# Six of 31 convolution taps as ScalarE products added up in DRAM, and no cleared probability blocks

## The chip, the cores and the metric

One core of one Trainium2 chip runs the whole kernel. Its engines work from queues of their own and meet through semaphores: TensorE (PE, matmuls), VectorE (DVE), ScalarE (ACT), GpSimd (POOL) and the DMA queues, of which SyncE (SP) issues nearly all here. The metric is device time in microseconds. Before the change it is 1760.06 us, the median of 3 runs (1760.02 to 1760.11).

## The reference

One layer of a decoder trunk on 1024 tokens of 1024 channels, all in float32. An input projection feeds two mixers; their gated sum goes through an output projection, and a SwiGLU block follows. What the change touches is the convolution branch and the weighting of the attention:

```python
p = probs(qb1, k1f) - lamf * probs(qb2, k2f)          # causal softmax, twice, per head
return jnp.einsum('bhqk,bhkd->bhqd', p, vf)
...
c = causal_depthwise_conv(u_a * jax.nn.sigmoid(u_b), conv_w[l], conv_b[l])   # width 31, per channel
c = jax.nn.silu(layer_norm(c, conv_ln_w[l], conv_ln_b[l]))
y_b = c @ w_proj_conv[l]
```

Per channel the convolution is a sum of 31 shifted copies of u, each times one number, plus a bias. The probabilities are causal: for a query block i, key blocks above i have weight zero.

## The kernel before

Every float32 matrix product is made of three float32r products (high times high, high times low, low times high; `mm3`, L152 to L154). So each operand is split: ScalarE casts the high part (`split_hi`, L119), VectorE subtracts to get the low part (`split_lo`, L124). `whi` and `wlo` are a weight's parts, made from the loaded `wraw`.

The first stage (`first`, L345) runs projection items one after the other: V (values), U (the two halves of the convolution's input) and the first head's Q. A U item makes one tile of 128 channels of u, as `sg`, and stores it to `u_d[c]` in DRAM. The convolution works on such tiles, c from 0 to 7: `conv_load` (L505) has POOL clear 30 columns of margin at the left of the tile `u` and SP load the rest; `conv_taps` (L514) is one VectorE operation per tap over 128x1024 elements, the first (L519) with the bias, 30 more (L525) that multiply and add into `acc`; SP stores `acc` to `c_d[c]`. There are two buffers of `u` and one of `acc`.

The taps are background work. The list `bg.todo` holds them, and `bg.step` emits a few after each piece of foreground work: 3.25 per yield of an item in the first stage (L764), and in attention as many as each step's slack allows (L970). Load number c goes into the list 31 places before its end (L551), that is, ahead of the taps of the tile before. A scheduler then places the emitted instructions on each engine's queue by its own timing, so the queues are not simply in the order of the source; `after(...)` only keeps an instruction behind another one.

Attention goes through 64 steps of a head and a block of 128 queries. `scores` (L798): PE multiplies into `sc` (three banks, L816 and L817), VectorE adds the bias and finds the minimum (`mn`, L818), ScalarE exponentiates and sums (`l`, L823), VectorE makes two reciprocals (L829, L833) and subtracts the second softmax from the first (L832). `turn` (L836) transposes the probabilities `E` into `pT` (L852) and splits them into `ph` and `pl`, which hold two query blocks, 256 columns, per key block. For the odd key block 2b+1 the first 128 of these columns lie above the diagonal; POOL clears them (L842, L843) in each new tile. `weigh` (L857) multiplies by the values `vh` and `vl` into `pW`, 256 columns for each key block; `back` (L869) turns the result back and scales it by the reciprocal in `RL`. Projection items (`more`, L910) fill PE's queue between these. The pool `a0` of the first stage (`ap`, with four buffers `xt` of x tiles) is closed at L771, and the attention tiles take its room.

The LayerNorm over channels (`ln_chunks`, L1020) loads all `c_d` after attention.

Of the kernel before, what the change touches and what calls it, by code (L numbers as in the profile page):

```python
# [56 lines left out]
def kernel(  # L57
# [456 lines left out]
    def conv_taps(c):  # L514
        acc = []

        def first_tap():
            acc.append(cv.tile([P, S], F32, tag="acc", name=f"acc{c}", bufs=1))
            dve.tensor_scalar(  # L519
                acc[0][:], us[c][:, 0:S], cw[:, c, 0:1], pcol("conv_b", c), op0=ALU.mult, op1=ALU.add  # L520
            )

        def tap(t):
            def go():
                dve.scalar_tensor_tensor(  # L525
                    acc[0][:], us[c][:, t : t + S], cw[:, c, t : t + 1], acc[0][:], op0=ALU.mult, op1=ALU.add
                )
                if t == CW - 1:
                    nc.sync.dma_start(c_d[c][:], acc[0][:])

            return go

        return [first_tap] + [tap(t) for t in range(1, CW)]
# [264 lines left out]
    def scores(h, i):  # L798
# [4 lines left out]
        l = sm.tile([P, 2], F32, tag="l", name=nm("l"))  # L803
        E = []
        qs = slice(i % 4 * P, (i % 4 + 1) * P)
        for j in range(2):
# [4 lines left out]
            for w in SPLITS[i]:  # L811
# [9 lines left out]
                )  # L821
                c0 += w
            act.activation(  # L823
                e[:, :nk], e[:, :nk], AF.Exp, bias=mn[:, j : j + 1], scale=-1.0, accum_out=l[:, j : j + 1]
            )
        if h not in RL:
            RL[h] = sm.tile([P, NT], F32, tag="rl1", name=f"rl1_{h}")
        c = sm.tile([P, 1], F32, tag="rl", name=nm("rl"))
        dve.reciprocal(c[:], l[:, 1:2])  # L829
        dve.scalar_tensor_tensor(c[:], c[:], neglam[:], l[:, 0:1], op0=ALU.mult, op1=ALU.mult)  # L830
        e1, e2 = E[0][:, :nk], E[1][:, :nk]
        dve.scalar_tensor_tensor(e1, e2, c[:], e1, op0=ALU.mult, op1=ALU.add)  # L832
        dve.reciprocal(RL[h][:, i : i + 1], l[:, 0:1])  # L833
        ES[h, i] = E[0]

    def turn(h, i):  # L836

        b = i // 2
        if (h, b) not in PT:
            ph = aps.tile([P, NT, 256], F32R, tag="ph", name=nm("ph"), bufs=1)  # L840
            pl = aps.tile([P, NT, 256], F32R, tag="pl", name=nm("pl"), bufs=1)
            pool.memset(f32(ph[:, 2 * b + 1, 0:P]), 0.0)  # L842
            pool.memset(f32(pl[:, 2 * b + 1, 0:P]), 0.0)  # L843
            PT[h, b] = ph, pl
        ph, pl = PT[h, b]
        e = ES.pop((h, i))
        qs = slice((i % 2) * P, (i % 2 + 1) * P)
        for k0 in range(0, i + 1, 4):
            n = min(4, i + 1 - k0)
            pt = pm("pT")  # L850
            for k in range(n):
                pe.transpose(pt[:, k * P : (k + 1) * P], e[:, (k0 + k) * P : (k0 + k + 1) * P], ident[:])  # L852
# [16 lines left out]
    def back(h, b, ar):  # L869
# [6 lines left out]
        jk = sm.tile([P, VD], F32, tag="jk", name=nm("jk"), bufs=1)  # L876
        for e in range(2):
            i = 2 * b + e
            src, r = pt[:, e * P : (e + 1) * P], RL[h][:, i : i + 1]
            act.activation(AN[h][:, i, :], src, AF.Identity, scale=r)  # L880
            act.activation(jk[:], src, AF.Square, scale=r, accum_out=SSA[h][:, i : i + 1])

# [638 lines left out]
```

## Time and profile before

| | us |
|---|---|
| median of the runs | 1760.06 |
| the profiled execution's own time | 1761.41 |
| its span in the profile | 1759.6 |
| VectorE busy in the span | 1273.2 |
| ScalarE busy in the span | 800.5 |

The span is one execution as the hardware profiler saw it, with 1.8 us of the execution's time outside. A row of a view gives busy time and the mean duration of one instruction; "idle before" is the time in which the engine stood still ahead of the instructions of that group, with the instruction that ended it. Matmuls are pipelined, so the distance from start to start tells their pace, not the duration in the row. The granted TensorE clock is full in every slice of the page.

### The profile page before, as it was taken

Reading aid. Unit: us, or ns where it says so; the run is one execution under the profiler, and the core shown is the slowest. Engines: PE = TensorE matmul, PEld = TensorE weight load, DVE = VectorE, ACT = ScalarE, POOL = GpSimd, SP = SyncE. Lnnn points to the kernel's source line nnn. Section 1 sums busy time; section 2 is a strip of 40 time slices with the busy share of each in tenths; the row PEclk is TensorE's granted clock in tenths of the full one; section 3 lists DMA queues with packets and bytes.
Section 4 is the critical chain, followed back from the end, with each engine's and each line's share of the span. In section 5 each row is a group of like instructions: output and inputs, shape, how many; then the busy total and the mean of one; then the engine's idle time right before and its main releaser. Section 6 shows DMA issues by size and latency. Waiting matters only on the chain.

```text
span 1759.6 us, 25844 instructions
## 1 busy us (share of the span) xinstructions
PE 1740.3 (99%) x9367; PEld 1503.1 (85%) x9367; DVE 1273.2 (72%) x2187; ACT 800.5 (45%) x1886; POOL 26.7 (2%) x106
## 2 busy tenths in 40 slices
PE   7999999999999999999999999999999999999999
PEld 6898998988999998988888888888888888888887
DVE  6388879999988888886687534877667666664544
ACT  4211241558767776655557313643333333333332
POOL 3000000000000000000000000000000000000000
PEclk9999999999999999999999999999999999999999
DMA  8433353235444344352983544234544544697663
GB/s 248 164 121 114 108 158 124 76 96 151 111 138 124 88 114 138 86 163 76 336 268 108 168 167 144 91 102 146 177 150 158 176 157 139 210 360 242 215 216 131
DMA packets 255728, 275.34 MB, mean 156 GB/s; under 512 B 16064, under 2 KB 177896, under 8 KB 255600
## 3 DMA queue, kind: packets, MB, share of 16 engines
q1 hardware_dynamic: 253568, 267.45, 47.6%
q0 software_dynamic: 1744, 5.19, 1.0%
q8 instruction: 74, 1.21, 0.3%
q10 hardware_dynamic: 288, 1.05, 0.2%
q14 instruction: 54, 0.44, 0.1%
HBM read 176.59 MB, written 78.68 MB: 145 GB/s over the span
## 4 chain that ended last, share of the span: by engine, by line
PE 95%; DMA 2%; ACT 1%; DVE 1%; issue 0%; SPq 0%; ACTq 0%
PE acc L1375 22%; PE pg L153 15%; PE pg L154 15%; PE pg L152 15%; PE acc L451 12%; PE sc L817 2%; PE sc L816 2%; PE wo L154 2%; PE wo L153 2%; PE wo L152 2%; PE pT L852 2%; PE pW L152 1%; PE pW L154 1%; PE pW L153 1%; PE pQ L714 1%; DMA wraw<-in_w_in_dram 1%
## 5 line engine op out<-in xcount | busy, mean ns | idle before, releaser
L525 DVE SCALAR_TENSOR_TENSOR acc<-u,cw,acc 128x1024 f32<-128x1024 f32 x240 | 306.8, 1278 | 2.8
L152 PE MATMUL pg<-whi,hT_hi 128*128 128x256 f32 x768 | 220.3, 287 | 1.2 <-ACT hT_hi L119 1.2
L154 PE MATMUL pg<-whi,hT_lo 128*128 128x256 f32 x768 | 219.8, 286 | 0.4 <-DVE hT_lo L124 0.4
L153 PE MATMUL pg<-wlo,hT_hi 128*128 128x256 f32 x768 | 219.1, 285 | 0.2 <-DVE wlo L124 0.2
L119 ACT CAST whi<-wraw 128x1024 fp32r<-128x1024 f32 x109 | 114.4, 1051 | 215.9 <-PE pg L153 122.1
L152 PE MATMUL pg<-hT_hi,whi 128*128 128x512 f32 x512 | 201.6, 394 | 0.0
L154 PE MATMUL pg<-hT_hi,wlo 128*128 128x512 f32 x512 | 200.9, 393 | 0.0
L153 PE MATMUL pg<-hT_lo,whi 128*128 128x512 f32 x512 | 200.5, 392 | 0.0
L124 DVE TENSOR_TENSOR wlo<-wraw,whi 128x1024 fp32r<-128x1024 f32 x109 | 132.8, 1219 | 70.8 <-ACT whi L119 66.7
L124 DVE TENSOR_TENSOR wlo<-draw,whi 128x1024 fp32r<-128x1024 f32 x75 | 91.8, 1224 | 89.6 <-ACT whi L119 84.3
L152 PEld LDWEIGHTS pg<-whi,hT_hi 128*128 128x128 f32 x768 | 147.7, 192 | 4.2 <-ACT hT_hi L119 2.5
L154 PEld LDWEIGHTS pg<-whi,hT_lo 128*128 128x128 f32 x768 | 147.8, 192 | 2.3 <-DVE hT_lo L124 1.1
L153 PEld LDWEIGHTS pg<-wlo,hT_hi 128*128 128x128 f32 x768 | 147.7, 192 | 2.0 <-DVE wlo L124 0.5
L119 ACT CAST whi<-draw 128x1024 fp32r<-128x1024 f32 x75 | 79.1, 1055 | 129.5 <-PE acc L451 125.9
L451 PE MATMUL acc<-wlo,whi 128*128 128x512 f32 x308 | 119.8, 389 | 0.0
L451 PE MATMUL acc<-whi,wlo 128*128 128x512 f32 x308 | 119.8, 389 | 0.0
L823 ACT ACTIVATE E<-E,mn 128x256 f32<-128x256 f32 (+7 forms) x128 | 99.7, 779 | 35.8 <-DVE mn L818 33.6
L154 PEld LDWEIGHTS pg<-hT_hi,wlo 128*128 128x128 f32 x512 | 96.2, 188 | 19.0
L153 PEld LDWEIGHTS pg<-hT_lo,whi 128*128 128x128 f32 x512 | 96.2, 188 | 18.7
L152 PEld LDWEIGHTS pg<-hT_hi,whi 128*128 128x128 f32 x512 | 96.3, 188 | 18.3
L1375 PE MATMUL acc<-h_hi,whi 128*128 128x512 f32 x240 | 93.4, 389 | 0.0
L1375 PE MATMUL acc<-h_lo,whi 128*128 128x512 f32 x240 | 93.4, 389 | 0.0
(270 smaller groups left out, 3951.5 us busy)
## 6 DMA issues: line engine op xcount, KB each, us to landing
wraw<-in_w_gate_up_dram SPq DMA_DIRECT2D x44, 512.0 KB, 4.8
wraw<-in_w_in_dram SPq DMA_DIRECT2D x40, 512.0 KB, 4.5
qs<-qs SPq DMA_DIRECT2D x96, 128.0 KB, 2.3
wd<-in_w_down_dram SPq DMA_DIRECT2D x44, 256.0 KB, 3.1
tdT<-wd SPq DMA_DIRECT2D x88, 128.0 KB, 4.3
draw<-sdS SPq DMA_DIRECT2D x44, 256.0 KB, 3.8
draw<-tdT SPq DMA_DIRECT2D x44, 256.0 KB, 3.9
wraw<-in_w_in_dram SPq DMA_DIRECT2D x32, 256.0 KB, 3.3
```

Of the source, the lines that this page charges most:

```text
L119: act.copy(dst, src)
L124: last_lo[0] = dve.tensor_tensor(dst, src, f32(hi), op=ALU.subtract).ins
L152: pe.matmul(o, lh, rh, start=start, stop=False)
L153: pe.matmul(o, lh, rl, start=False, stop=False)
L154: last_mm[0] = pe.matmul(o, ll, rh, start=False, stop=stop).ins
L451: m = pe.matmul(o[s_][i][:], l_[:, ts], r_[:, 512:], start=start and j + y_ == 0, stop=j == n - 1 and y_ == 2, skip_group_check=not start,)
L525: dve.scalar_tensor_tensor(acc[0][:], us[c][:, t : t + S], cw[:, c, t : t + 1], acc[0][:], op0=ALU.mult, op1=ALU.add)
L816: pe.matmul(o[:, :w], qh[:, qs], k, start=True, stop=False)
L817: last_mm[0] = pe.matmul(o[:, :w], ql[:, qs], k, start=False, stop=True).ins
L823: act.activation(e[:, :nk], e[:, :nk], AF.Exp, bias=mn[:, j : j + 1], scale=-1.0, accum_out=l[:, j : j + 1])
L852: pe.transpose(pt[:, k * P : (k + 1) * P], e[:, (k0 + k) * P : (k0 + k + 1) * P], ident[:])
L1375: pe.matmul(o[:], a_[x_][:, k, :], b_[y_][:, k, :], start=start and k + x_ + y_ == 0, stop=k == 3 and x_ == 1, skip_group_check=not start,)
```

## The change

For the tiles c = 0 to 4 (`FROM_ACT` = 5), taps 0 to 5 (`ADDED` = 6) are not done by VectorE. ScalarE makes each product in a buffer `part` (of the four `xt` buffers). POOL's queue stores the first one, with the bias, to `c_d[c]`, and adds the others to it with accumulating DMAs. VectorE starts at tap 6, emits one product after every fourth of its taps, and writes its last tap into `u` itself, from where POOL's queue adds it to `c_d[c]`, too. Tiles 5 to 7 keep all their taps on VectorE. The margin of `u` is cleared by VectorE now.

In `weigh` the last key block is multiplied for the second 128 columns alone, so `ph` and `pl` need no cleared block. The sums of the first softmax go straight into `RL`, and one reciprocal is made for two query blocks.

```diff
+    ADDED, FROM_ACT = 6, 5
...
-            pool.memset(u[:, : CW - 1], 0.0)
+            dve.memset(u[:, : CW - 1], 0.0)
             nc.sync.dma_start(u[:, CW - 1 :], u_d[c][:])
...
+        def product(t):
+            with after(last_of(mybir.EngineType.Activation)):
+                part_ = ap.tile([P, S], F32, tag="xt", name=nm("part"), bufs=4)
+                u, w = us[c][:, t : t + S], cw[:, c, t : t + 1]
+                if t == 0:
+                    act.activation(part_[:], u, AF.Identity, scale=w, bias=pcol("conv_b", c))
+                    pool.dma_start(c_d[c][:], part_[:])
+                else:
+                    act.activation(part_[:], u, AF.Identity, scale=w)
+                    pool.dma_start(c_d[c][:], part_[:], accum_op=ALU.add)
...
         def tap(t):
             def go():
-                dve.scalar_tensor_tensor(
-                    acc[0][:], us[c][:, t : t + S], cw[:, c, t : t + 1], acc[0][:], op0=ALU.mult, op1=ALU.add
-                )
+                u, w = us[c][:, t : t + S], cw[:, c, t : t + 1]
+                if t == n_add:
+                    acc.append(cv.tile([P, S], F32, tag="acc", name=f"acc{c}", bufs=1))
+                    if n_add:
+                        dve.tensor_scalar(acc[0][:], u, w, None, op0=ALU.mult)
+                    else:
+                        dve.tensor_scalar(acc[0][:], u, w, pcol("conv_b", c), op0=ALU.mult, op1=ALU.add)
+                else:
+
+                    dst = us[c][:, :S] if t == CW - 1 else acc[0][:]
+                    dve.scalar_tensor_tensor(dst, u, w, acc[0][:], op0=ALU.mult, op1=ALU.add)
+                if (t - n_add) % 4 == 3 and (t - n_add) // 4 < n_add:
+                    product((t - n_add) // 4)
                 if t == CW - 1:
-                    nc.sync.dma_start(c_d[c][:], acc[0][:])
+                    if n_add:
+                        pool.dma_start(c_d[c][:], us[c][:, :S], accum_op=ALU.add)
+                    else:
+                        nc.sync.dma_start(c_d[c][:], us[c][:, :S])
...
-                bg.todo.insert(max(0, len(bg.todo) - CW), conv_load(c))
-                bg.add(conv_taps(c))
+                n_add = ADDED if c < FROM_ACT else 0
+                bg.todo.insert(max(0, len(bg.todo) - CW + n_add), conv_load(c))
+                bg.add(conv_taps(c, n_add))
...
-        dve.reciprocal(RL[h][:, i : i + 1], l[:, 0:1])
+        if i % 2:
+            dve.reciprocal(RL[h][:, 1, i - 1 : i + 1], RL[h][:, 0, i - 1 : i + 1])
...
-            pool.memset(f32(ph[:, 2 * b + 1, 0:P]), 0.0)
-            pool.memset(f32(pl[:, 2 * b + 1, 0:P]), 0.0)
...
-            mm3(o[:, :256], vh[:, k, :], vl[:, k, :], ph[:, k, :], pl[:, k, :], k == 0, k == nkt - 1)
+            q = slice(P if k == nkt - 1 else 0, 256)
+            mm3(o[:, q], vh[:, k, :], vl[:, k, :], ph[:, k, q], pl[:, k, q], k == 0, k == nkt - 1)
```

With 30 taps fewer in the list, the queues come out otherwise. POOL's queue after the bias rows held only clears before, first of `u`, then of `ph` and `pl`:

```order
L677 DMA t_d7_330<-b_d_322 128x1152
L508 MEMSET u2_1485 128x30
L508 MEMSET u3_1869 128x30
L842 MEMSET ph_285_3217 128x128
L843 MEMSET pl_286_3218 128x128
L508 MEMSET u4_2431 128x30
```

Now it holds the stores and accumulations, here from the first of tile 0 to the third of tile 1:

```order
L527 DMA c_d0_160<-part_95_996 128x1024
L530 DMA c_d0_160<-part_97_1030 128x1024
L530 DMA c_d0_160<-part_100_1064 128x1024
L530 DMA c_d0_160<-part_111_1168 128x1024
L530 DMA c_d0_160<-part_115_1230 128x1024
L530 DMA c_d0_160<-part_119_1292 128x1024
L527 DMA c_d1_161<-part_134_1413 128x1024
L530 DMA c_d1_161<-part_136_1448 128x1024
L549 DMA c_d0_160<-u0_949 128x1024
L530 DMA c_d1_161<-part_139_1482 128x1024
```

Each accumulation on one `c_d` waits for the one before it, and tile 0's last (L549) stands behind two transfers of tile 1.

VectorE's queue where one tile's taps end and the next one's begin (`wlo` and `sg` belong to the projection items) read before:

```order
L525 SCALAR_TENSOR_TENSOR acc0_952<-u0_949,cw_114,acc0_952 128x1024 x3
L548 TENSOR_TENSOR sg_130_1453<-pg_131_1458,sg_130_1453 128x512
L124 TENSOR_TENSOR wlo_134_1494<-wraw_132_1491,whi_133_1493 128x1024
L519 TENSOR_SCALAR acc1_1424<-u1_1085,cw_114,pvec_105 128x1024
L525 SCALAR_TENSOR_TENSOR acc1_1424<-u1_1085,cw_114,acc1_1424 128x1024 x5
L548 TENSOR_TENSOR sg_139_1528<-pg_140_1534,sg_139_1528 128x512
```

and reads now:

```order
L544 SCALAR_TENSOR_TENSOR u0_949<-u0_949,cw_114,acc0_952 128x1024
L570 TENSOR_TENSOR sg_133_1410<-pg_135_1418,sg_133_1410 128x512
L538 TENSOR_SCALAR acc1_1369<-u1_1094,cw_114 128x1024
L544 SCALAR_TENSOR_TENSOR acc1_1369<-u1_1094,cw_114,acc1_1369 128x1024 x2
L124 TENSOR_TENSOR wlo_131_1382<-wraw_129_1379,whi_130_1381 128x1024
L544 SCALAR_TENSOR_TENSOR acc1_1369<-u1_1094,cw_114,acc1_1369 128x1024
L510 MEMSET u2_1512 128x30
L544 SCALAR_TENSOR_TENSOR acc1_1369<-u1_1094,cw_114,acc1_1369 128x1024 x2
```

The last tap goes into `u0`, and the clear of `u2`, in the same buffer, follows after four taps and two other operations.

At the start of attention, where VectorE's first score reduction (L818 before, L844 now, `E` from `sc` and `tb0`) stands in its queue, the taps before it belonged to tile 4:

```order
L525 SCALAR_TENSOR_TENSOR acc4_2876<-u4_2431,cw_114,acc4_2876 128x1024
L548 TENSOR_TENSOR sg_254_2980<-pg_255_2985,sg_254_2980 128x512
L818 ISA E_258_3036,mn_256_3034<-sc_259_3037,tb0_3032 128x128
L818 ISA mn_256_3034 128x1
L818 ISA E_260_3042,mn_256_3034<-sc_261_3043,tb0_3032 128x128
```

Now tile 4 is done, tile 5 has begun, and the clear of `u6` stands just ahead:

```order
L544 SCALAR_TENSOR_TENSOR u4_2064<-u4_2064,cw_114,acc4_2681 128x1024
L540 TENSOR_SCALAR acc5_2972<-u5_2823,cw_114,pvec_105 128x1024
L124 TENSOR_TENSOR wlo_279_2986<-wraw_277_2982,whi_278_2985 128x1024
L544 SCALAR_TENSOR_TENSOR acc5_2972<-u5_2823,cw_114,acc5_2972 128x1024
L233 TENSOR_TENSOR neglam_130<-lsum_132 128x1
L544 SCALAR_TENSOR_TENSOR acc5_2972<-u5_2823,cw_114,acc5_2972 128x1024
L510 MEMSET u6_2969 128x30
L234 TENSOR_SCALAR neglam_130<-neglam_130 128x1
L544 SCALAR_TENSOR_TENSOR acc5_2972<-u5_2823,cw_114,acc5_2972 128x1024
L570 TENSOR_TENSOR sg_284_3074<-pg_285_3079,sg_284_3074 128x512
L844 ISA E_288_3131,mn_286_3128<-sc_289_3132,tb0_3126 128x128
```

The reductions write `E` into a buffer of `part`, and the loads of `vh0`, `vl0` and `tb0` on SP go into such buffers, too.

More of the change, by code (lines that the diff above doesn't have):

```diff
@@ L512, in conv_load, with conv_taps @@
         return go
-    def conv_taps(c):
+    def conv_taps(c, n_add):
         acc = []
[L517 to L520, printed above, removed]
-            )
+        def product(t):
[8 more added lines that the diff above has]
+                    pool.dma_start(c_d[c][:], part_[:], accum_op=ALU.add)
         def tap(t):
             def go():
-                dve.scalar_tensor_tensor(
-                    acc[0][:], us[c][:, t : t + S], cw[:, c, t : t + 1], acc[0][:], op0=ALU.mult, op1=ALU.add
-                )
+                u, w = us[c][:, t : t + S], cw[:, c, t : t + 1]
[10 more added lines that the diff above has]
+                    product((t - n_add) // 4)
                 if t == CW - 1:
-                    nc.sync.dma_start(c_d[c][:], acc[0][:])
+                    if n_add:
+                        pool.dma_start(c_d[c][:], us[c][:, :S], accum_op=ALU.add)
+                    else:
+                        nc.sync.dma_start(c_d[c][:], us[c][:, :S])
             return go
-        return [first_tap] + [tap(t) for t in range(1, CW)]
+        return [tap(t) for t in range(n_add, CW)]
     hT_hi = big.tile([P, NKT, S], F32R, tag="xhi", name="hT_hi")
@@ L802, in scores @@
         mn = sm.tile([P, 2], F32, tag="mn", name=nm("mn"))
-        l = sm.tile([P, 2], F32, tag="l", name=nm("l"))
+        l = sm.tile([P, 1], F32, tag="l", name=nm("l"))
+        if h not in RL:
+            RL[h] = sm.tile([P, 2, NT], F32, tag="rl1", name=f"rl1_{h}", bufs=2)
+        l0 = RL[h][:, 0, i : i + 1]
         E = []
@@ L823, in scores @@
             act.activation(
-                e[:, :nk], e[:, :nk], AF.Exp, bias=mn[:, j : j + 1], scale=-1.0, accum_out=l[:, j : j + 1]
+                e[:, :nk], e[:, :nk], AF.Exp, bias=mn[:, j : j + 1], scale=-1.0, accum_out=l[:] if j else l0
             )
-        if h not in RL:
-            RL[h] = sm.tile([P, NT], F32, tag="rl1", name=f"rl1_{h}")
         c = sm.tile([P, 1], F32, tag="rl", name=nm("rl"))
-        dve.reciprocal(c[:], l[:, 1:2])
-        dve.scalar_tensor_tensor(c[:], c[:], neglam[:], l[:, 0:1], op0=ALU.mult, op1=ALU.mult)
+        dve.reciprocal(c[:], l[:])
+        dve.scalar_tensor_tensor(c[:], c[:], neglam[:], l0, op0=ALU.mult, op1=ALU.mult)
         e1, e2 = E[0][:, :nk], E[1][:, :nk]
         dve.scalar_tensor_tensor(e1, e2, c[:], e1, op0=ALU.mult, op1=ALU.add)
-        dve.reciprocal(RL[h][:, i : i + 1], l[:, 0:1])
+        if i % 2:
+            dve.reciprocal(RL[h][:, 1, i - 1 : i + 1], RL[h][:, 0, i - 1 : i + 1])
         ES[h, i] = E[0]
@@ L878, in back @@
             i = 2 * b + e
-            src, r = pt[:, e * P : (e + 1) * P], RL[h][:, i : i + 1]
+            src, r = pt[:, e * P : (e + 1) * P], RL[h][:, 1, i : i + 1]
             act.activation(AN[h][:, i, :], src, AF.Identity, scale=r)
```

## The prediction

> **What bounds the kernel now.** I read the page first, then the windows by stage, then TensorE's (PE's) waits, then the starts of single matmuls.
>
> ```profile
> span 1759.6 us, 25844 instructions
> PE 1740.3 (99%) x9367; PEld 1503.1 (85%) x9367; DVE 1273.2 (72%) x2187; ACT 800.5 (45%) x1886; POOL 26.7 (2%) x106
> ...
> PE 95%; DMA 2%; ACT 1%; DVE 1%; issue 0%; SPq 0%; ACTq 0%
> ```
>
> The span is a line of matmuls: PE is busy for 99% of it and 95% of the chain that ended last is PE. A change to the other engines is therefore worth only what PE waits for them. The next table cuts the span at the start of the convolution's taps (80 us), at attention's first score reduction (319 us) and at attention's end (826 us); the second counts the taps alone (L525).
>
> ```profile
> core 0: us, PE busy (x) PEld busy (x) DVE busy (x) ACT busy (x) POOL busy (x), PEclk, DMA share, GB/s
> 0.00:80.00 80.00, 68.71 (x403) 59.58 (x404) 40.40 (x103) 33.18 (x59) 14.15 (x35) 1.00 0.71 223
> 80.00:319.00 239.00, 239.00 (x1429) 214.13 (x1428) 202.90 (x193) 55.21 (x125) 0.85 (x6) 1.00 0.39 123
> 319.00:826.00 507.00, 503.48 (x3401) 461.19 (x3400) 449.70 (x1042) 345.51 (x1187) 11.73 (x65) 1.00 0.40 114
> 826.00:1760.00 934.00, 929.15 (x4140) 768.25 (x4138) 580.22 (x851) 366.55 (x516) 0.00 (x0) 1.00 0.55 182
> ...
> 80.00:319.00 239.00, 155.04 (x121) 1.00 0.39 123
> 319.00:826.00 507.00, 151.76 (x119) 1.00 0.40 114
> ```
>
> From 80 to 319 us PE has no idle time at all: nothing can be won there, only lost. Attention is where the change can earn: VectorE (DVE) is busy for 449.7 of 507 us (89%) and PE idles 507.00 - 503.48 = 3.5 us. Whom it waits for:
>
> ```profile
> PE sc L816 <- DVE mn L818: 0.8, 1, 0.8
> PE pW L152 <- DVE t L577: 0.6, 1, 0.6
> PE pB L872 <- DVE pl L124: 0.5, 1, 0.5
> PE sc L816 <- DMA ks<-klo: 0.5, 1, 0.5
> PE pW L152 <- DMA vh<-v_hi: 0.5, 1, 0.5
> PE pW L152 <- ACT jk L881: 0.3, 1, 0.3
> PE pT L852 <- DVE pl L124: 0.2, 1, 0.2
> ```
>
> The first of them in the timeline, PE's rows and then DVE's:
>
> ```profile
> 394.73 0.38 PE L872 MATMUL pB<-ident,ar 128*128 128x128 f32 x2
> 395.87 0.50 PE L816 MATMUL sc<-ks,qs 128*128 128x512 f32 x1 [0.75 <-DVE mn L818]
> 396.20 0.40 PE L817 MATMUL sc<-ks,qs 128*128 128x512 f32 x1
> ...
> 394.07 1.28 DVE L525 SCALAR_TENSOR_TENSOR acc<-u,cw,acc 128x1024 f32<-128x1024 f32 x1
> 395.27 0.15 DVE L829 RECIPROCAL rl<-l 128x1 f32<-128x1 f32 x1
> 395.34 0.14 DVE L833 RECIPROCAL rl<-l 128x1 f32<-128x1 f32 x1
> 395.40 0.40 DVE L818 CUSTOM_DVE_ANT_0 E<-sc,tb 128x256 f32<-128x256 f32 x1
> ```
>
> A tap of 1.28 us stands ahead of the reduction that frees PE's score bank. This wait costs more than its 0.75 us: two 128-wide transposes at some 0.11 us each (below) would have let the score start at 394.95, not 395.87 (0.92 us), and the next matmul follows after 0.33 us where 512 columns usually take 0.23 (0.10 more): 0.27 us on top of the idle time.
>
> **The change part by part.** Taps. Six of 31 taps leave DVE for five tiles of channels: 30 of 240 three-operand taps. By the order of the changed program 123 of the remaining 210 stand ahead of the first score reduction, against 121 of 240 before, so the first stage keeps its DVE load and attention's falls from 119 taps to 87.
>
> ```profile
> L525 DVE SCALAR_TENSOR_TENSOR acc<-u,cw,acc 128x1024 f32<-128x1024 f32 x119 | 151.8, 1275 | 0.0
> ...
> L833 DVE RECIPROCAL rl<-l 128x1 f32<-128x1 f32 x64 | 10.0, 156 | 3.0 <-ACT E L823 2.7
> ```
>
> 32 x 1.275 = 40.8 us, and 32 of the 64 reciprocals of L833, 32 x 0.156 = 5.0 us, leave attention: DVE goes from 449.7 to about 404 us, 80% of the stage. Of PE's seven waits, four have DVE's backlog in front of them (0.8, then 0.3 right behind it, 0.6 behind the root whose last step is L577, and 0.5 before the score at 634 us, which I put down to the same queue): 2.2 us idle, with 4 x 0.27 us on top 3.3 us. The two waits for pl (0.5 and 0.2) are the end of attention, where no tap is left, and vh is a load: they stay. The bounds are 0 (the waits come back elsewhere, since the order is a new one) and 3.5 + 7 x 0.27 = 5.4 us (all go). I take 3.0 us, near the 3.3, since a quarter of the taps less leaves a tap ahead of a reduction less often, not never.
>
> Half-wide products. In weigh the last key block of each pair of query blocks is now multiplied by 128 columns, not 256: 32 pairs x 3 = 96 matmuls. What such a matmul takes, with weights of its own:
>
> ```profile
> 441.62 0.28 PE L153 MATMUL pg<-wlo,hT_hi 128*128 128x256 f32 x1
> 441.74 0.22 PE L816 MATMUL sc<-ks,qs 128*128 128x128 f32 x1
> 441.81 0.28 PE L817 MATMUL sc<-ks,qs 128*128 128x128 f32 x1
> 441.92 0.33 PE L154 MATMUL pg<-whi,hT_lo 128*128 128x256 f32 x1
> 442.09 0.28 PE L152 MATMUL pg<-whi,hT_hi 128*128 128x256 f32 x1
> 442.21 0.29 PE L153 MATMUL pg<-wlo,hT_hi 128*128 128x256 f32 x1
> ...
> 394.30 0.60 PE L852 MATMUL pT<-ident,E 128*128 128x128 f32 x4
> ```
>
> 256 columns take 0.12 us from start to start (442.09 to 442.21). Two of 128 and the 256 behind them take 442.09 - 441.74 = 0.35 us, hardly less than three of 256 (0.36): the weights, not the columns, set the pace. The four transposes from 394.30 to 394.73 give 0.11 us each. So 96 x 0.01 = 0.9 us are saved; the bounds are 0 and half the time, 96 x 0.06 = 5.8 us. Against this stands the Trainium skill, "TensorE: Matmul & The Clock Gate", section "Back-to-back issue gap", which gives some 81 ns for a sustained stream of 128-wide matmuls with their loads; by that figure the saving would be about 3.7 us, an estimate that the rows above contradict. The cleared blocks (64 of POOL's 65 fills in attention, 0.2 us each) wait on PE and nobody on PE's list waits for them: 0, and at most 0.2 us a pair if the casts behind them were late.
>
> Products. 30 activations of 128x1024 on ScalarE (ACT), all in the first stage:
>
> ```profile
> L823 ACT ACTIVATE E<-E,mn 128x1024 f32<-128x1024 f32 x16 | 18.5, 1156 | 3.2 <-DVE mn L818 2.9
> ...
> t_d<-b_d POOLq DMA_DIRECT2D x8, 576.0 KB, 12.4
> u<-u_d SPq DMA_DIRECT2D x8, 512.0 KB, 4.8
> c_d<-acc SPq DMA_DIRECT2D x8, 512.0 KB, 3.0
> ...
> 34.28 4.12 POOL L677 DMA_DIRECT2D t_d<-b_d  x8 [2.01 <-DMA b_d<-gr]
> DMA to landing us min/median/max: 5.0/12.4/16.1
> ```
>
> 30 x 1.156 = 34.7 us on an engine that is busy for 55.2 of 239 us there; the cover is ACT's waiting for PE. Without it a product would hold up the cast of a weight by 1.2 us, against 10.9 us of matmuls (48 x 0.227, a set of 128 columns) for which the next set must be ready.
>
> The accumulating DMAs are the unknown. No row shows one. Each reads SBUF and DRAM and writes DRAM. From below: the plain store of the same tile, 3.0 us. From above: load and store one after the other, 4.8 + 3.0 = 7.8 us, or the eight queued POOL transfers, 12.4. The nearest row is the first of those (POOL's queue, DRAM read and written, 576 KB): 5.0 us. I take 6, with 0.52 us (4.12 / 8) to issue. The Trainium skill ("Collectives: The Full Stack", "The bandwidth ceiling: the fold count and why AG ≠ RS ≠ AR") says that an adding transfer needs two source reads and moves half as much as a copy; no run here shows it yet, and by it the 4.8 us load would become some 7 to 9 us.
>
> POOL issues them in order and each waits for the one before on the same c_d. A tile's chain is the plain first store (3.0 + 0.5), four accumulations awaited (4 x 6.5) and one more issue, about 31 us; the fifth lands beside the next tile's first store. A tile has 239 x 25/123 = 48.6 us. So the chain fits up to (48.6 - 4) / 4 - 0.5 = 10.6 us a transfer. Up to there neither POOL nor ACT (a product waits for the transfer of four products ago) holds anything up.
>
> The added waits: DVE now clears u's margin, and that clear waits until the accumulation that read the tile of two before has landed. Queued behind it on DVE are taps, wlo splits and the gate products (for which PE's banks wait), on SP's queue behind the load of u the weight loads. The worst placed is u6's clear: after u4's last tap DVE does a first tap (0.81), a split (1.22) and two taps, about 4.6 us, and the landing comes 6.5 us after the tap: 1.9 us of waiting, just ahead of the first score reductions. u2, u3 and u5 have four to six taps and a wait for PE in between, u4 a root on ACT: 0 to 2 us each. DVE has 239 - 203 = 36 us to spare in this stage, and the wait of L519 for acc's store goes:
>
> ```profile
> DVE acc L519 <- DMA c_d<-acc: 7.1, 4, 3.3
> ```
>
> So 5 x 2 us at most are added and 7 taken away; PE, with four banks and weights two sets ahead, sees 0 (bounds: 0, and 2 us at attention's start). Also there, SP's loads of vh0, vl0 and tb0 lie in the room of the product tiles and wait for the last two products' transfers; the order gives them some ten taps (13 us) against 2 x 6.5.
>
> **Sum**: -3.0 - 0.9 + 0 = -3.9 us. The profiled execution took 1761.41 us (span 1759.6 and 1.8 around it), 1.35 above the median of 1760.06; it would become 1757.5, and the median **1756.2 us**. What this kernel's measurement tells from no change is about 0.2%, 3.5 us: the forecast lies just beyond it.
>
> **Rivals.** (B) The waits only move: 32 fewer taps, but a new order on every engine, so new waits of the same size appear, or 1.9 us at attention's start give the gain back. For it: seven waits of 0.2 to 0.8 us are accidents of an order. Against: DVE at 80% has twice the slack. Time: 1760.06 - 0.9 = 1759.2.
> (C) Slower: the accumulating transfer is long, and the clears of u, in order on DVE, wait for it. At 10 us, u6's clear waits 10.5 - 4.6 = 5.9 us with the first score reductions behind it, and PE, which has one group of fill there (48 x 0.12 = 5.8 us, already spent on DVE's own work), waits as long; u2's, u3's and u5's wait 4 to 5 us each, of which I let PE see a third, 5 us: 1760.1 - 3.9 + 5.9 + 5 = 1767. From 10.6 us on the chain decides: at 12.4 us a tile takes 4 + 4 x 12.9 = 55.6 us, 7 too many, five times 35 us, less about 10 for the four product buffers: 1760 - 4 + 25 = 1781. It decides from about 9 us. For it: the 12.4 row, and PE without idle time to lose there. Against: 5.0 us for the first in the queue.
> (D) The narrow matmuls take half their time and all seven waits go: -5.8 - 5.4 = 1748.9. Against it stand the rows at 441 us. The skill's 81 ns with my 3.0 us gives 1753.4, between (D) and the forecast.
>
> **Chances.** Forecast 0.45 (own range 1754 to 1758.5), B 0.25, C 0.20, D 0.10. Faster by over 0.2% (below 1756.5): nearly seven tenths of the forecast and D, 0.41. Slower by over 0.2% (above 1763.6): C, and 0.02 of B: 0.22. Within: 0.37. The range from 1752.5 to 1767 leaves out half of D and the long-transfer half of C.
>
> **What would show it.** Taps in attention 87, DVE near 404 us there, PE's waits there below 2 us without "DVE mn"; pW matmuls of 128 columns 0.11 us apart; accumulations landing in 5 to 8 us; PE still without idle time up to 319 us. It is wrong if PE waits before 319 us or at the first scores (then C), if transfers land after more than 10 us, or if the narrow matmuls are 0.06 us apart (D).

## The result and the profile after

The changed kernel takes 1766.45 us, the median of 6 runs (1765.27 to 1769.21), against 1760.55 us of the kernel before beside it (6 runs, 1760.02 to 1761.68): a ratio of 1.0033, 95% interval 1.0023 to 1.0043. It is a third of a per cent slower; faster was forecast. On a second chip it took 1764.57 against 1760.90 us, 1.0022 (1.0013 to 1.0032).

The profiled execution took 1766.18 us, 4.8 us more than that of the kernel before. Its page, three lines:

```profile
span 1764.4 us, 25707 instructions
PE 1740.1 (99%) x9367; PEld 1503.3 (85%) x9367; DVE 1241.1 (70%) x2133; ACT 833.8 (47%) x1916; POOL 42.9 (2%) x69
...
PE 75%; DVE 4%; DMA 3%; ACT 1%; issue 1%; SPq 0%; POOL 0%; DVEq 0%; ACTq 0%; POOLq 0%
```

PE does the same number of matmuls, and VectorE is busy 32 us less. But the chain that ended last, 95% PE before, is 75% PE now. Two of the windows, cut as for the kernel before, and last the taps alone (L544):

```profile
core 0: us, PE busy (x) PEld busy (x) DVE busy (x) ACT busy (x) POOL busy (x), PEclk, DMA share, GB/s
80.00:319.00 239.00, 239.00 (x1426) 214.00 (x1425) 199.17 (x193) 86.16 (x154) 27.83 (x34) 1.00 0.79 187
319.00:826.00 507.00, 499.28 (x3380) 457.56 (x3379) 421.61 (x987) 346.23 (x1182) 1.07 (x2) 1.00 0.40 114
...
319.00:826.00 507.00, 115.83 (x91) 1.00 0.40 114
```

The first stage still has no idle PE, with 31 us more on ACT (55.2 before) and twice the DMA share. Attention lost 28 us of VectorE's work, and PE idles there for 507.00 - 499.28 = 7.7 us where it idled for 3.5. For whom it waits in the whole span, the column behind the name being the total, the times and the longest:

```profile
PE px L639 <- DVE xt L636: 9.4, 1, 9.4
PE pW L152 <- DMA vh<-v_hi: 2.2, 3, 1.5
PE pT L875 <- DVE E L856: 1.8, 1, 1.8
PE px L639 <- issue: 1.5, 1, 1.5
PE pg L152 <- ACT aTh L119: 1.4, 1, 1.4
PE pT L875 <- DVE pl L124: 1.0, 1, 1.0
PE sc L842 <- DVE mn L844: 1.0, 1, 1.0
PE pg L153 <- DVE wlo L124: 0.7, 1, 0.7
```

The first is the start of the kernel, as before. Of the others only the last two, scores and a product with `wlo`, wait for VectorE's queue. A load, the last transposes of attention and the first cast behind it are the larger ones, and the 1.5 us of "issue" stand at the start of the kernel (last section).

**The start of attention.** VectorE's timeline from the last tap of tile 3 (272.40, written into u) to the clear of u5's margin (L510):

```profile
272.40 1.28 DVE L544 SCALAR_TENSOR_TENSOR u<-u,cw,acc 128x1024 f32<-128x1024 f32 x1
...
288.88 0.08 DVE L510 MEMSET u<- 128x30 f32 x1 [8.77 <-DMA c_d<-u]
```

POOL's queue in the same time:

```profile
275.11 0.85 POOL L530 DMA_DIRECT2D c_d<-part  x1 [8.40 <-DMA c_d<-part]
280.88 0.86 POOL L530 DMA_DIRECT2D c_d<-part  x1 [4.92 <-issue]
281.42 1.20 POOL L549 DMA_DIRECT2D c_d<-u  x1
```

The tile was finished at 273.7 us. Its accumulation (L549) was issued at 281.42, because two additions of tile 4 stood ahead of it on POOL. By the times the second of these waited for the first to land, and the first had waited for tile 4's plain first store: this was issued at 265.84, 0.5 us behind an accumulation, and landed 8.8 us later, where such a store takes 3.1 by the median. Tile 3's own accumulation landed at 288.8. The clear of u5, in order on VectorE, stood still for 8.77 us. VectorE had this time to spare, but not the time to make it good before attention:

```profile
271.00:290.00 19.00, 19.00 (x86) 15.73 (x85) 9.91 (x11) 5.49 (x7) 3.46 (x4) 1.00 0.81 163
290.00:319.00 29.00, 29.00 (x130) 24.01 (x129) 28.47 (x26) 7.28 (x9) 1.72 (x2) 1.00 0.76 201
319.00:328.00 9.00, 7.28 (x58) 6.83 (x57) 7.88 (x15) 1.29 (x2) 0.86 (x1) 1.00 0.72 146
```

(columns as above; VectorE's busy time is the third value after the bare length). It works for 28.5 of the next 29 us, and PE stands still for 1.7 us of the first nine of attention: once for a weight's split, and once for the first reductions, ahead of which u6's clear waits again:

```profile
322.02 0.39 PE L153 MATMUL pg<-wlo,hT_hi 128*128 128x256 f32 x1 [0.71 <-DVE wlo L124]
...
325.56 0.08 DVE L510 MEMSET u<- 128x30 f32 x1 [1.08 <-DMA c_d<-u]
...
327.39 0.28 DVE L844 CUSTOM_DVE_ANT_0 E<-sc,tb 128x128 f32<-128x128 f32 x1
```

**The end of attention.** The last head's last block, changed kernel:

```profile
818.76 0.75 DVE L844 CUSTOM_DVE_ANT_0 E<-sc,tb,mn 128x512 f32<-128x512 f32 x1 [2.80 <-PE sc L843]
819.56 1.15 ACT L849 ACTIVATE E<-E,mn 128x1024 f32<-128x1024 f32 x1 [0.93 <-DVE mn L844]
819.96 0.93 PE L875 MATMUL pT<-ident,E 128*128 128x128 f32 x7
821.29 1.28 DVE L856 SCALAR_TENSOR_TENSOR E<-E,rl,E 128x1024 f32<-128x1024 f32 x1
822.72 0.63 PE L875 MATMUL pT<-ident,E 128*128 128x128 f32 x4 [1.83 <-DVE E L856]
824.36 0.66 PE L875 MATMUL pT<-ident,E 128*128 128x128 f32 x4 [1.02 <-DVE pl L124]
```

And the kernel before:

```profile
815.61 0.49 PE L852 MATMUL pT<-ident,E 128*128 128x128 f32 x3
815.86 0.36 PE L152 MATMUL pW<-ph,vh 128*128 128x256 f32 x1
...
816.97 1.28 DVE L832 SCALAR_TENSOR_TENSOR E<-E,rl,E 128x1024 f32<-128x1024 f32 x1
...
818.10 1.28 PE L852 MATMUL pT<-ident,E 128*128 128x128 f32 x8
```

In both, the last reduction, the exponential, two small operations and the merge of the softmaxes (1.28 us) take some 4 us after the last scores. Before, PE does the last weighing but one (18 matmuls `pW` from 815.86) in this time. In the changed order this weighing starts at 815.98, ahead of the last two score matmuls (818.05), and only six fill matmuls and seven transposes are left for that time. VectorE's backlog has no part in it: at 818.76 it had been idle for 2.8 us.

**All kernels in one table.** To compare orders, I add up over a stretch what each matmul's start is behind the usual distance to the one before it (0.227, 0.177, 0.120 and 0.110 us after one of 512, 384, 256 and 128 columns, from the traces); unlike idle time this has the slow starts after a wait in it. Medians are device times; ratios are to the kernel before on the same chip (1760.55 to 1761.13 us there). The four columns on the right come from the one profiled execution of each kernel, which can lie off its median: that of e1 took 1767.00 us, the longest of its 11 runs. One run of a2 took 4325.66 us and is left out of its ratio.

| kernel | median us | ratio (95%) | lost 0-320 | 320-360 | 360-800 | 800-880 |
|---|---|---|---|---|---|---|
| before | 1760.55 | 1 | 7.1 | 0.1 | 6.0 | 3.1 |
| changed | 1766.45 | 1.0033 (1.0023-1.0043) | 8.0 | 2.7 | 5.7 | 6.1 |
| changed, again | 1764.57 | 1.0022 (1.0013-1.0032) | 7.2 | 1.9 | 5.8 | 7.7 |
| e1 attention edits only | 1763.35 | 1.0013 (1.0004-1.0022) | 7.2 | 0.1 | 9.6 | 5.5 |
| e2 taps only | 1767.27 | 1.0027 (1.0017-1.0037) | 8.0 | 2.0 | 5.9 | 6.4 |
| e3 taps left out | 1762.25 | 1.0005 (0.9996-1.0014) | 7.6 | 0.2 | 2.6 | 7.0 |
| e4 margins cleared once | 1763.12 | 1.0006 (0.9997-1.0015) | 7.1 | 0.1 | 4.7 | 7.5 |
| e5 full width | 1766.45 | 1.0033 (1.0022-1.0043) | 8.0 | 1.7 | 4.4 | 7.5 |
| e6 = e4, weighing later | 1761.40 | 1.0004 (0.9995-1.0013) | 8.2 | 0.2 | 4.5 | 5.9 |
| e7 = e6, V from POOL | 1765.07 | 1.0026 (1.0016-1.0036) | 9.6 | 0.1 | 5.9 | 7.4 |
| n1 before, pace 3.20 | 1770.74 | 1.0048 (1.0034-1.0061) | 9.0 | 0.0 | 13.4 | 4.6 |
| n2 before, pace 3.40 | 1763.18 | 1.0012 (1.0003-1.0021) | 7.0 | 0.0 | 4.5 | 6.0 |
| c4 before, fill kept | 1769.73 | 1.0045 (1.0032-1.0058) | 10.0 | 0.1 | 12.8 | 2.8 |
| a1 changed, pace 3.20 | 1762.32 | 1.0004 (0.9995-1.0013) | 7.3 | 1.5 | 1.0 | 7.0 |
| a2 changed, pace 3.40 | 1760.57 | 0.9999 (0.9990-1.0008) | 8.1 | 0.5 | 1.8 | 5.6 |
| d2 changed, fill kept | 1760.91 | 0.9997 (0.9988-1.0006) | 9.5 | 2.3 | 3.2 | 2.6 |
| c3 = e4, fill kept | 1755.35 | 0.9967 (0.9955-0.9980) | 6.6 | 0.1 | 1.2 | 3.0 |
| d1 = c3, pace 3.40 | 1755.15 | 0.9966 (0.9953-0.9978) | 6.5 | 0.1 | 1.6 | 2.2 |

The changed kernel against the one before: +0.9, +2.6, -0.3 and +3.0 us, 6.2 in all; the narrow matmuls give about 1 back, since the sum counts from their own usual distance. That is near the 4.8 us of span. The gain in the middle of attention did not come, and two places of 2.6 and 3.0 us were added.

### The profile page after: what moved, and what is told of

It reads as the page before. It is cut to its first block, busy times and chain, and to the rows that moved or that the text cites. A ratio compares the mean times of both kernels' runs of the same rounds, so it can differ in the third digit from the quotient of the medians.

```text
span 1764.4 us, 25707 instructions
## 1 busy us (share of the span) xinstructions
PE 1740.1 (99%) x9367; PEld 1503.3 (85%) x9367; DVE 1241.1 (70%) x2133; ACT 833.8 (47%) x1916; POOL 42.9 (2%) x69
## 4 chain that ended last, share of the span: by engine, by line
PE 75%; DVE 4%; DMA 3%; ACT 1%; issue 1%; SPq 0%; POOL 0%; DVEq 0%; ACTq 0%; POOLq 0%
PE acc L1400 22%; PE acc L453 12%; PE pg L153 9%; PE pg L152 9%; PE pg L154 9%; DVE acc L544 2%; PE sc L843 2%; PE sc L842 2%; PE wo L153 2%; PE wo L152 2%; PE wo L154 2%; PE pT L875 1%; PE pW L154 1%; PE pW L153 1%; PE pW L152 1%
## 5 line engine op out<-in xcount | busy, mean ns | idle before, releaser
L544 DVE SCALAR_TENSOR_TENSOR acc<-u,cw,acc 128x1024 f32<-128x1024 f32 x202 | 258.3, 1279 | 2.6
```

Source lines behind the costliest of these rows:

```text
L544: dve.scalar_tensor_tensor(dst, u, w, acc[0][:], op0=ALU.mult, op1=ALU.add)
```

## Experiments

**Round one: parts of the change.** Theory 1 says that new waits at a few places cost the time; theory 2 that the accumulating transfers do. e1 is the kernel before with the attention hunks of the diff, e2 with the hunks on the taps. e3 is the changed kernel without the six products of the five tiles, so its convolution lacks these taps; e4 is the changed kernel with the margins cleared once. Their edits, e3's first:

```diff
-                    product((t - n_add) // 4)
+                    pass
...
-                    if n_add:
-                        pool.dma_start(c_d[c][:], us[c][:, :S], accum_op=ALU.add)
-                    else:
+                    if True:
                         nc.sync.dma_start(c_d[c][:], us[c][:, :S])
```

```diff
-            u = cv.tile([P, S + CW - 1], F32, tag="u", name=f"u{c}", bufs=2)
-            dve.memset(u[:, : CW - 1], 0.0)
+            if c < 2:
+                u2.append(cv.tile([P, S + CW - 1], F32, tag=f"u{c}", name=f"u{c}", bufs=1))
+                dve.memset(u2[c][:, : CW - 1], 0.0)
+            u = u2[c % 2]
...
-                    dst = us[c][:, :S] if t == CW - 1 else acc[0][:]
+                    dst = us[c][:, CW - 1 :] if t == CW - 1 else acc[0][:]
```

(in e4 the stores then read `us[c][:, CW - 1 :]`.) What was expected, in this order:

> The kernel before with the attention edits alone (half-wide last key block, no cleared blocks, paired reciprocals); all 31 taps stay on VectorE. Theory 1, the loss sits in new waits at places (attention's start with u6's clear, the load of vh at 465 us, the end of attention at 820 us), and the one at the end of attention comes with the attention edits' order: the end still idles PE 3 us, and the time is 1759 to 1762. Theory 2, the accumulating transfers cost the time: without them only the gain of the narrow matmuls is left, 1757.5 to 1759.5, and PE's stalls are those of the kernel before.

> The kernel before with the taps' edit alone (30 products on ScalarE, accumulating transfers, clears of u on VectorE); products of full width and cleared blocks stay. Theory 1: the waits at attention's start (2 us) and perhaps at 465 us (1.5 us) come, that at the end of attention doesn't: 1761 to 1764. Theory 2: the whole loss and the lost saving of the narrow matmuls, 1766 to 1768.

> The changed kernel with the six products of the five tiles, and every transfer that adds, left out: the convolution of these tiles lacks six taps, and a tile's one store is plain. VectorE and the attention edits as in the changed kernel. Theory 1: u6's clear and the loads of vh0 wait for no transfer, so the start of attention is some 2 us shorter, while the waits at 465 and 820 us stay: 1762 to 1765. Theory 2: all of the loss goes and the forecast gain shows, 1755 to 1759.

> The changed kernel with two fixed buffers for u, whose margins are cleared once, since the last tap is written beside the margin and not over it; no clear of u waits for an accumulation then. Theory 1: the wait ahead of the first score reductions goes, 1.5 to 2.5 us, so 1764 to 1765. Theory 2: transfers stay as they are, 1766, within 0.5 us of the changed kernel.

e1 took 1763.35 us, above what either theory gave: the attention edits, which add no work and no transfer, lose time by themselves. The end idles as theory 1 said (5.5 lost against 3.1), and in the profiled execution, a long one, 3.6 us more are lost in the middle, most in two waits of scores for copies of q and k:

```profile
PE sc L819 <- DMA qs<-qs: 1.8, 1, 1.8
PE pT L852 <- DVE pl L124: 1.4, 1, 1.4
...
PE sc L819 <- DMA ks<-klo: 1.1, 1, 1.1
```

e2, 1767.27 us, fits theory 2 by its time, but not by its places: 2.0 us at attention's start, and 3.3 more at the end, where no accumulation has run for some 500 us. Theory 1 missed here, too: it put the wait at the end down to the attention edits, and e2 has it without them. e3 has no product and no added transfer and still isn't faster than the kernel before (1762.25): its start of attention and its middle are good, its end loses 7.0. So theory 2 falls for all but the start of attention. e4 keeps all 30 adding transfers and takes 0.9 us more than e3, 1763.12, with intervals that overlap. The start of attention is clean in it, and in e3, which has the clears but no adding transfer: so that loss takes both, a clear that waits for a late accumulation. The table bears this out at every order: the seven kernels with both lose 0.5 to 2.7 us from 320 to 360, the others at most 0.2. e4's windows:

```profile
271.00:290.00 19.00, 19.00 (x86) 15.72 (x85) 18.51 (x17) 4.61 (x5) 3.46 (x4) 1.00 0.84 161
...
319.00:328.00 9.00, 9.00 (x77) 9.00 (x77) 8.31 (x18) 4.40 (x23) 0.00 (x0) 1.00 0.43 142
```

VectorE is busy for 18.51 of the 19 us in which that of the changed kernel worked for 9.91, and PE loses nothing up to 328 us. e4 takes all the clears' waits away at once, so it doesn't part u5's share from that of u6's.

**Round two: the places.** e5 is the changed kernel with full-width products; e6 is e4 with the weighing put later; e7 is e6 with another queue in `load_v`; in this order:

```diff
+            pool.memset(f32(ph[:, 2 * b + 1, 0:P]), 0.0)
+            pool.memset(f32(pl[:, 2 * b + 1, 0:P]), 0.0)
...
-            q = slice(P if k == nkt - 1 else 0, 256)
+            q = slice(0, 256)
```

```diff
-                weighs.append((n, (hp, ip // 2)))
+                weighs.append((n + (n == len(steps) - 2), (hp, ip // 2)))
```

```diff
-            nc.sync.dma_start(
+            pool.dma_start(
```

> The changed kernel itself, for comparison on one chip with the three runs beside it: 1765 to 1768, and the stalls of its first trace at the same places (2.5 us around 321 to 327 us, 1.5 at 465, 3 at the end of attention, 1.5 at 851).

> The changed kernel with full-width products in weigh and the cleared blocks back; the taps and the reciprocals as changed. By the forecast's term a narrow matmul saves 0.01 us: 0.9 us more than the changed kernel. By the starts in the changed kernel's trace (0.061, 0.115 and 0.110 us for the three, against 3 x 0.12) it saves 0.07 us a pair, less what the matmul behind them loses: up to 2.4 us more. If the order of the queues decides instead, the difference is anything from -2 to +4 us and sits in a few stalls.

> The changed kernel with the margins of u cleared once and, besides, the one before the last weighing put behind the last scores, so that its 18 matmuls lie between the last scores and the transposes that wait for VectorE's last merge. Theory 1 (the end of attention idles since nothing is left between those two): the two stalls of 2.0 and 1.2 us at 816 to 819 us go, and the time is 2 to 3 us below that with the margins cleared once, 1760 to 1761.5. If the end is bound by the chain on ScalarE and VectorE whatever stands between: no change, 1763.

> As the run with the end mended, and the loads of vh and vl issued by POOL, whose queue is empty in attention, not by SP behind the copies of q and k. Theory 1 (the wait for vh at 465 us is a place in SP's queue): the 1.4 us go, 1758.5 to 1760. If the load is late because the buffer comes free late: no change.

The changed kernel came out at 1764.57, just below the expected range, with its stalls at the same places. e5 is 1.9 us slower, with intervals that overlap and another order, so the narrow matmuls are better read from the trace (below). e6 reached 1761.40, as expected and 1.7 below e4, though the intervals overlap: the wait for the merge went, but the last transposes now wait 2.2 us for `pl`, since the scheduler also put a weight's cast and split ahead of the last exponential and merge. e7 is a miss: the vh wait at 465 us went, and waits for qs (2.5 us in three) and a late vh (1.0) came, with vh landing 5.9 us after its issue on POOL, not 4.2.

**Round three: is it the order?** By now each change of the queues had made new waits at other places, the edits without any work of their own too. Theory 3 is that the kernel before has a good order among many. n1 and n2 change one number of the kernel before, with the same instructions; c3 takes one step of fill out of the last head and leaves it for the end; c4 is its control. n1 (n2 has 3.4), and then the edit of c3 (on e4) and c4 (on the kernel before):

```diff
-    TAPS_FIRST = 3.25
+    TAPS_FIRST = 3.2
```

```diff
+    plan[7] -= 1
     last_fill = [None]
```

> The kernel before, with 3.20 taps per yield in the first stage where it has 3.25; every instruction is the same, only the order of the queues changes. Theory 3 (the queues' order of the kernel before is a good one among many, and whatever changes it costs): PE stalls at the end of attention as in the changed kernel (3 us against 1.5), with a few stalls elsewhere, 1761.5 to 1764. If the loss belongs to the change's own instructions: 1760.5 to 1761.3, as before.

> The same with 3.40 taps per yield, a second neutral order. Theory 3: 1761.5 to 1764.5, with PE idle at the end of attention. If the loss belongs to the change's own instructions: 1759.5 to 1761.3, a little less than before perhaps, since nine taps more leave attention.

> The changed kernel with the margins cleared once and one step of the projection fill (24 matmuls of 512 columns, 5.4 us of PE) taken out of the last head's steps and left for the end of attention, where it runs behind the last scores. By the order the weighing before the last one then lies between the last scores and the last transposes, as before. Theory (the changed order placed the last scores some 4 us later and so left less work of PE behind them to cover the chain to the last head's result; VectorE's relief can be used to run attention with less fill): the stalls of 3.2 us at the end and 1.5 us at 851 us go, 1758 to 1760. If other waits come in their place: 1762 to 1764.

> The kernel before with that same edit, one step of fill left for the end; as control. All taps stay on VectorE, and by the order the end now has the weighing ahead of 15 transposes, as the changed kernel has it. If the relief of VectorE is what makes the edit pay: more waits in attention than before, 1762 to 1764. If leaving fill to the end pays by itself: 1757 to 1760.

n1 costs 9.9 us, more than I expected of it, with nothing in it but another order (two taps more fall behind 319 us):

```profile
PE sc L816 <- DMA qs<-qs: 1.9, 1, 1.9
PE sc L816 <- DMA ks<-klo: 1.6, 1, 1.6
```

These are the kinds of waits that e1 has. n2 costs 2.3 us, and it corrects the reading of the end: the 18 matmuls `pW` lie behind its last scores, as in the kernel before, and PE still waits for the merge, since a weight's cast and a gate's activation stand ahead of the last exponential on ACT, as in e6:

```profile
818.59 1.17 PE L852 MATMUL pT<-ident,E 128*128 128x128 f32 x8 [1.57 <-DVE E L832]
```

So the end depends on what ScalarE and VectorE do ahead of the last block as well as on what is left for PE. c4, the fill step alone, costs 8.9 us, beyond both of its ranges. Its loss is in the middle (12.8), with n1's two waits:

```profile
PE sc L816 <- DMA qs<-qs: 2.0, 1, 2.0
...
PE sc L816 <- DMA ks<-klo: 1.4, 1, 1.4
```

A control at one order, it therefore can't tell a poor order from what the fill step does without VectorE's relief. c3, the same edit on the changed kernel with once-cleared margins, gives 1755.35 us, faster than foreseen and than the kernel before. Its attention, and its largest waits but the start's 9.4:

```profile
319.00:826.00 507.00, 505.44 (x3424) 464.88 (x3423) 416.59 (x983) 349.14 (x1195) 0.21 (x1) 1.00 0.40 113
...
PE px L641 <- issue: 1.2, 1, 1.2
PE pT L877 <- ACT ph L119: 0.9, 1, 0.9
```

**Round four: like orders.** The one comparison missing was the change at other orders, and a second order for the fastest. a1 is the changed kernel at a pace of 3.2, a2 at 3.4, d1 is c3 at 3.4; d2 is the changed kernel with c3's edit of the plan, without e4's.

```diff
-    TAPS_FIRST = 3.25
+    TAPS_FIRST = 3.4
```

> The changed kernel with 3.20 taps per yield in the first stage, a neutral order, as the kernel before had it (1770.7 there). If the loss against the kernel before is that one's good order: at or below 1767, so not slower than the kernel before at the same number. If the change itself costs: 1768 or more.

> The changed kernel with 3.40 taps per yield (the kernel before: 1763.2). If the order decides: 1762 to 1768, around the changed kernel's own 1764.6 to 1766.5, with less spread than the kernel before shows, since VectorE has slack. If the change itself costs 4 us or more: above 1767.

> The fastest so far (margins cleared once, one fill step left for the end) with 3.40 taps per yield. By its order the end has the weighing ahead of 15 transposes again. If the fill left for the end pays through the work behind the last scores: the wait at the last transposes grows to 2 to 3 us, and the rest stays, 1757 to 1759.5. If it was one lucky order: 1761 or more.

> The changed kernel with the fill step left for the end, the margins of u cleared each time as changed. By theory the wait ahead of the first score reductions (2 to 2.5 us) is added to 1755.4: 1757 to 1758.5. If the fill step's gain hung on the order that the clears made: 1761 or more.

One number doesn't make the queues of two kernels alike; each number is one more order for both. At pace 3.20 the changed kernel takes 1762.32 us where the kernel before takes 1770.74; at 3.40, 1760.57 against 1763.18. Only at 3.25 is the change slower. Over the three numbers the kernel before spreads over 10 us and the changed one over 4 to 6. On the mean of the three ratios the changed kernel is ahead by 1.4 to 2.1 us, less than either spread: three orders don't settle what the change is worth by itself. In the middle of attention, where the forecast had put its gain, a1 and a2 lose 1.0 and 1.8 us against 13.4 and 4.5: there the gain is. d1 gives 1755.15 at another order, so c3 is not one lucky order. But its last transposes wait 0.6 us, not the 2 to 3 foreseen, so why the fill step helps the end stays open. d2, without the once-cleared margins, is at 1760.91, above the range foreseen: the 2.3 us at attention's start are back, with some 2 us in the middle, and its profiled execution had a poor start as well.

## Why the prediction was wrong

The forecast was -3.9 us, and the profiled executions lie 4.8 apart the other way. Three terms failed: the -3.0 for PE's waits in attention, of which 0.3 came, and the zeros for attention's start (2.6 lost) and its end (3.0 lost).

- **The step that gave the sign** was -3.0 us for PE's waits in attention, with 0 as the bound "the waits come back elsewhere, since the order is a new one". The bound is what happened at this order: 6.0 lost between 360 and 800 us before, 5.7 after. The named wait at 395 us did go, and taps in attention fell as counted (91 from 319 us on, of which four ran ahead of the late first reduction; the 87 foreseen in e4, where no clear waits); loads of vh and v's low part (2.2 and 0.4 us of waits) took the place. I had treated a reorder as a loss of at most the gain. n1 shows that it can cost 10 us. At paces 3.20 and 3.40 the changed kernel does lose less there than the kernel before, 12.4 and 2.7 us, by one profiled execution each.
- **"The two waits for pl ... are the end of attention, where no tap is left ...: they stay."** This failed, by 3.0 us (3.1 to 6.1 lost from 800 to 880). That no tap is there says nothing about which matmuls stand between the last scores and the last transposes. The changed order was on hand, and I had read it at attention's start only.
- **"u2, u3 and u5 have four to six taps and a wait for PE in between ...: 0 to 2 us each."** u5's clear waited 8.77 us, and the five such waits came to 13.7 us where 10 were the most foreseen. The transfer was as long as bounded (7.4 us); what I left out is the place on POOL behind two chained additions of the next tile and that tile's first store of 8.8 us, put at 3.0, although I had named that queue. From the last tap to the landing it took 288.88 - 273.68 = 15.2 us, not 6.5. The cover (36 us of VectorE's slack in the stage) was right for the sum and wrong for the place: 30 us before attention's first reductions. For attention's start I had put 0, with 2 us as the bound: 1.7 us of idle time came, 2.6 with the slow starts.
- **Right: the accumulating transfers.** I took 6 us, to land in 5 to 8:

```profile
L530 POOL DMA_DIRECT2D c_d<-part x25: 851/860/905, 85.5 to 299.2; - x25
...
DMA to landing us min/median/max: 5.3/5.7/8.1
```

  (min, median and max of the issue in ns, then of the landing in us; the last ones of a tile took 5.2/7.4/9.2.) The issue was 0.86 us, not 0.52. The plain first stores of the same tile landed in 3.1 us by the median, so adding takes 1.8 times as long. The Trainium skill ("Collectives: The Full Stack", "The bandwidth ceiling: the fold count and why AG ≠ RS ≠ AR") puts a ring's reduce-scatter at half the rate of an all-gather, since the add needs two source reads. The 1.8 is near that for another kind of transfer; that a second read is the reason here, no run shows.
- **Right: the products.** 31 us came to ACT before 319 us (34.7 foreseen), and PE had no idle time there.
- **Right: the narrow matmuls.** The last key block's three, in the changed kernel:

```profile
817.77 0.22 PE L152 MATMUL pW<-ph,vh 128*128 128x128 f32 x1
817.83 0.28 PE L153 MATMUL pW<-pl,vh 128*128 128x128 f32 x1
817.95 0.27 PE L154 MATMUL pW<-ph,vl 128*128 128x128 f32 x1
818.05 0.44 PE L842 MATMUL sc<-ks,qs 128*128 128x512 f32 x1
818.34 0.39 PE L843 MATMUL sc<-ks,qs 128*128 128x512 f32 x1
```

  The three take 0.28 us, not 0.36, but the score behind them takes 0.29, not 0.23: 0.57 against 0.59 from the first of the three to the second score, and 0.42 against 0.47 to the second transpose where transposes follow. Over 32 pairs that is 0.6 to 1.6 us; 0.9 was forecast. By the Trainium skill ("TensorE: Matmul & The Clock Gate", "Back-to-back issue gap") 128-wide matmuls come 81 ns apart; here the three are followed after 61, 115 and 110 ns in the median of the 32, and the matmul behind the next one is late, so the figure doesn't hold for these float32r matmuls.
- **The size of VectorE's relief** was off: 404 us foreseen, 415.7 in e4 with exactly the 87 taps. The groups' own busy times fall by the 45.8 us of the forecast (40.8 of taps, 5.0 of reciprocals), but neighbours on VectorE overlap by up to 0.1 us in these rows (a tap of 1.28 us starts at 276.50 and the split behind it at 277.69), so the stage's busy time falls by 34.

Of the rivals, B (the waits only move, 1759.2) had the mechanism, and C had the place: clears in order on VectorE behind a late accumulation, at a smaller size. The result lies between the two. What neither had is that the order of the kernel before was worth 2.3 and 9.9 us over the two neighbours that were run, so that an edit is likely to lose by the new order alone. Why the scheduler's queues come out well or badly at a given number, no run shows.

## What to carry to other kernels

- Where a scheduler sets the queues of a kernel that has been tuned to 99% on one engine, compare a change at several neutral orders (a pace, a position) of both kernels; one order each measures luck. Here the same work spread over 10 us.
- Count a wait on a queue's end from the work that precedes it there, chained transfers included, and ask where the next deadline is. Better, take the wait away: a margin that nothing overwrites needs clearing once.
- Ask where the relief of a helper engine can be spent: here by giving attention less fill and keeping it for the end. The version with margins cleared once and one step of fill kept is 0.33% faster than the kernel before (1755.35 us, ratio 0.9967, 0.9955 to 0.9980), and as much at a second order. That it takes the relief is argued and not shown: the same edit without it is 0.45% slower, but at one order only, and by waits that n1 has without the edit.

## What the runs showed of the hardware

The start of the kernel varies from run to run, and the mean granted clock with it. In the changed kernel's profile PE reached its full pace at 15.3 us (0.12 us a matmul of 256 columns), stood still for 1.5 us from 16.5, and then ran at 0.21 us a matmul until 24.3:

```profile
16.22 0.28 PE L154 MATMUL pg<-whi,hT_lo 128*128 128x256 f32 x1
17.97 1.94 PE L639 MATMUL px<-ident,xt 128*128 128x128 f32 x8 [1.46 <-issue]
...
22.12 0.41 PE L152 MATMUL pg<-whi,hT_hi 128*128 128x256 f32 x1
22.33 0.41 PE L153 MATMUL pg<-wlo,hT_hi 128*128 128x256 f32 x1
```

The granted clock in the window from 20 to 25 us was 0.55. The kernel before has such matmuls 0.21 us apart, too, at its very start, up to 18.4 us, but there the granted clock is given as 1.00, so that clock alone doesn't tell the pace. Of 31 runs of the kernel before on one chip, the 14 with a mean clock of 1.000 had a median span of 1758.7 us and the six with 0.998 one of 1761.4. That the short stop brought the lower clock is read from the order of events; no run tested it. It also leaves some of the differences above to chance: a microsecond or so between medians, and more between single profiled executions.
